# A 31-tap depthwise convolution moved from POOL to TensorE, and most of the weight splits moved from DVE to POOL

## The chip, the cores and the metric

One core of one Trainium2 chip runs the whole program. The metric is the device time of one execution in microseconds. The kernel before takes 1408.82 us (median of 3 runs, 1407.81 to 1412.9). DVE is VectorE, ACT is ScalarE, POOL is GpSimd, PE is TensorE, SP is the engine whose queue issues the transfers.

## What is computed

One transformer layer on 256 tokens of 1024 channels, all in float32: one input projection feeds three mixers (latent attention, a Mamba-2 scan, a convolution module), their outputs are gated, merged and projected, and then a mixture of 32 experts follows. The part that the change rewrites is the convolution module:

```python
CNV_CH, CNV_WIDTH, SEQ = 512, 31, 256

def _conformer_conv(a, gt, dw_w, dw_b, ln_g, ln_b):
    u = a * jax.nn.sigmoid(gt)
    u = _dwconv(u, dw_w, dw_b)          # each channel by its own 31 taps, centred
    return jax.nn.silu(_layernorm(u, ln_g, ln_b))
```

Every channel is filtered alone: out[c, t] = b[c] + sum over j of w[j, c] * u[c, t + j - 15].

## The kernel before

**The weights.** All matrices ahead of the experts are cut on the host into 696 blocks of 128x128, and eight blocks make a unit (`unit(u)`, 512 KB, 87 units). A unit is loaded into a `raw` buffer (three of them), copied by ACT into a rounded float32r half `wh` (L242), and the rest `wl` = raw - wh is taken by a subtraction of 128x1024 (L243), called a split below. L243 runs on DVE, or on POOL where the unit's number stands in `LOW_POOL` (17 units, the first is 47). `wh` and `wl` have three buffers each. PE then does three matmuls per block (L286 to L288: wh by the high half of the input, wh by its low half, wl by the high half).

**The order.** PE's order is written out by hand in `SEQ`: each word is one step, and a step that is named again goes on to its next phase. The other engines' instructions are ordered by a scheduler. Every engine runs its own list in order. The first part of SEQ holds the projections for the convolution (cnv), attention (cq, cqn, qk, att), the Mamba inputs (x), then the scan (ssd), the norms, the gates (g), the convolution's layer norm (conf) and the merged outputs (br). The order of the blocks follows SEQ, so the units do too.

**The convolution.** `do_cnv(c)` treats 128 channels (c from 0 to 3). Its first phase projects a, its second projects the gate and writes u into `ups` with 15 zeros on either side (L382, DVE). Then POOL does all 31 taps: one multiplication with bias (L384), and 30 times a product (L387) and a sum (L388), 128x256 each. The result, `cacc`, is first read by `do_conf` (`fold`, L356, on DVE).

**The experts.** While the mixers run, the first experts' weights are loaded into a ring of tiles (`do_pre`, sent between units). From about 420 us on, the 32 experts follow, with a megabyte per tile and 12 tiles per expert.

Of the kernel before, what the change touches and what calls it, by code (L numbers as in the profile page):

```python
# [18 lines left out]
P = 128  # L19
# [19 lines left out]
NR = (11, 12, 14, 18, 19)  # L39
SLOTS = (9, 10, *range(9), *range(11, NR[4]))  # L40
XK = 2
LOW_POOL = (47, 49, 50, 51, 52, 54, 55, 56, 58, 61, 64, 65, 70, 73, 74, 75, 80)
MANUAL = {mybir.EngineType.PE}

OFF = dict(cq=0, ckv=384, kr=640, z=672, xbc=1696, dt=3232, a=3264, g=3776,
# [5 lines left out]


SEQ = """
cnv0 cnv0 cq1 cq2 cnv1 cq4 cq0 cq3 cnv1 kr0 cqn0 cnv2 dt0 cqn0 cnv3 kr0 cqn0 cnv3 x1 qk2 qk0 x9
att0 x10 qk1 cnv2 v0 x0 att0 x5 qk3 dt0 x2 att1 att0 dt0 x11 att2 att1 x8 pre0 att1 x6 att3 att2
x4 x3 pre1 att2 att3 x7 mid0 att3 pre2 pre3 ssd0 z2 ssd0 ssd0 z1 z4 ssd0 ssd1 ssd1 z0 ssd1 g1 z5
z3 ssd1 nrm0 ssd2 nrm1 nrm0 ssd2 pre4 g1 g0 ssd2 g1 g0 nrm0 nrm1 z6 ssd2 ssd3 z7 g4 g3 nrm2 ssd3
nrm2 conf0 g4 pre5 pre6 conf0 nrm1 conf0 g2 g3 g0 conf0 ssd3 g2 conf0 g3 g5 ssd3 conf0 nrm3 g4
# [7 lines left out]
def _plan():  # L66
# [7 lines left out]

    for kind, i in ORDER + [("out", 0)]:
        ph = phase[kind, i] = phase.get((kind, i), -1) + 1
        if kind == "cnv":
            proj(OFF["ag"[ph]] + i * P)
        elif kind == "g":
# [46 lines left out]
def _vec_plan():  # L126
    n = 0
    for name, w in (("b_g", 4), ("b_z", 8), ("b_gc", 8), ("b_ga", 8), ("b_gs", 8), ("cw5", 60), ("cb5", 12),
                    ("cw31", 124), ("clg", 4), ("clb", 4),
                    ("b_a", 4), ("b_xbc", 12), ("b_cq", 3), ("b_ckv", 2), ("b_kr", 1), ("cb31", 4),  # L130
                    ("qn", 3), ("kvn", 2), ("sn", 8), ("sd", 8), ("bbc", 8), ("lng", 8), ("lnb", 8)):
        VEC[name] = (n, w)
        n += w
    return n
# [43 lines left out]
def tile_trunk(ctx, tc, xT_d, xn_d, wf_d, vec_d, row_d, rw_d, cst_d, cst2_d, rope_d, ln1_d, ln2_d,  # L178
# [137 lines left out]
    def tmp(name, shape=None, tag="t1", bufs=4, dt=F32, pool=None):  # L316
        return (pool or m1).tile(shape or [P, S], dt, tag=tag, name=name, bufs=bufs)

    ups, cpr = slot(5, "ups", [P, 4 * (S + 30) + 2 * S]), None
    ups, cpr = ups[:, 0:4 * (S + 30)].rearrange("p (c n) -> p c n", c=4), ups[:, 4 * (S + 30):]  # L320
    PO.memset(ups[:, :, 0:15], 0.0)
    PO.memset(ups[:, :, S + 15:S + 30], 0.0)
    cbc = slot(6, "cbc", [P, 8, S])
    cacc, bmat, cmat = cbc[:, 0:4], cbc[:, 4:6], cbc[:, 6:8]
    xps = [m0.tile([P, S + 4], F32, name=f"xp{c}") for c in range(3)]
# [1 line left out]
        PO.memset(u_[:, 0:2], 0.0)  # L327
        PO.memset(u_[:, S + 2:S + 4], 0.0)
    xs = slot(7, "xs", [P, 8, S])
    sz = slot(8, "sz", [P, 8, S])  # L330
    vkt = slot(4, "vkt", [P, 6 * S])
    vt = vkt[:, 0:4 * S].rearrange("p (c n) -> p c n", c=2)
    krr, tab = vkt[:, 4 * S:5 * S], vkt[:, 5 * S:6 * S]
# [39 lines left out]
    def do_cnv(c):  # L373
# [6 lines left out]
        A.activation(th, pg, AF.Tanh, bias=W("b_g", c), scale=0.5)  # L380
        up = ups[:, c]
        V.scalar_tensor_tensor(up[:, 15:S + 15], th, 1.0, at, op0=ALU.add, op1=ALU.mult)  # L382
        acc = cacc[:, c]
        PO.tensor_scalar(acc, up[:, 0:S], W("cw31", c * 31), W("cb31", c), op0=ALU.mult, op1=ALU.add)  # L384
        for j in range(1, 31):
            pr = cpr[:, j % 2 * S:(j % 2 + 1) * S]
            PO.tensor_tensor(pr, up[:, j:j + S], W("cw31", c * 31 + j).to_broadcast([P, S]), op=ALU.mult)  # L387
            PO.tensor_add(acc, acc, pr)  # L388

    def do_x(t):  # L390
        px = proj(f"px{t}")
# [91 lines left out]

    def do_z(t):
        pz = proj(f"pz{t}")
        th = tmp(f"zth{t}")
        A.activation(th, pz, AF.Tanh, bias=W("b_z", t), scale=0.5)
        zv = tmp(f"zv{t}")
        A.activation(zv, pz, AF.Identity, bias=W("b_z", t), scale=0.5)
        V.scalar_tensor_tensor(sz[:, t], th, 1.0, zv, op0=ALU.add, op1=ALU.mult)  # L490
# [137 lines left out]

    def do_norm(g):
        y = ys[g]  # L630
        V.tensor_mul(y, y, sz[:, 2 * g:2 * g + 2])
        sq = tmp(f"ysq{g}", [P, 2, S], tag="ysq", bufs=1, pool=m2s[0])
        A.activation(sq, y, AF.Square)
        V.tensor_add(sq[:, 0], sq[:, 0], sq[:, 1])
# [95 lines left out]
            eng.dma_start(t, wdn_v[e, (u - 8) // 2, u % 2])  # L730
        return t

    nx, m2s, ys, dts, gths, att, mx, late = [0], [], [], [], {}, {}, [], {}
    steps = dict(cnv=do_cnv, x=do_x, dt=do_dt, cq=do_cq, kr=do_kr, cqn=do_cqn, z=do_z, v=do_v, qk=do_qk,
                 att=do_att, mid=do_mid, ssd=do_ssd, nrm=do_norm, conf=do_conf, g=do_g, pre=do_pre, br=do_br)
    live = {}
# [752 lines left out]
def pack(inputs):  # L1489
# [22 lines left out]
    put("b_kr", np.concatenate([kr, _swap(kr), np.tile(b[OFF["dt"]:OFF["dt"] + NE], 2)])[:, None])  # L1512
    put("cw5", f["ssm_conv_w"][0].reshape(5, 12, P).transpose(2, 1, 0).reshape(P, 60))
    put("cb5", cols(f["ssm_conv_b"][0]))
    put("cw31", f["cnv_dw_w"][0].reshape(31, 4, P).transpose(2, 1, 0).reshape(P, 124))
    put("cb31", cols(f["cnv_dw_b"][0]))
    put("clg", cols(f["cnv_ln_g"][0]))
    put("clb", cols(f["cnv_ln_b"][0]))
# [40 lines left out]
```

## Time and profile before

| | |
|---|---|
| median of 3 runs | 1408.82 us |
| the profiled execution's own time | 1414.25 us |
| its span, first to last instruction | 1412.4 us |
| mean granted TensorE clock | 0.902 of full speed |
| busy: PE, DVE, ACT, POOL | 1169.7, 614.1, 328.1, 293.4 us |
| POOL's products and sums of the convolution (L387, L388) | 100.6 and 124.4 us |
| splits on DVE (72) and on POOL (17) | 98.9 and 41.6 us |
| moved by DMA | 456.39 MB, 323 GB/s over the span |

The span has two halves with different limits. Up to about 390 us the mixers run, with little DMA in the first 250 us. From about 420 us to the end the experts run, with the DMA engines busy 99% of the time at 414 to 416 GB/s. The averages above mix the two, so the views below are taken by stretches of the first half. An engine's busy time holds the time in which one of its instructions had started and was held up.

### The profile page before, as it was taken

What the parts mean: (1) busy time and instruction counts of PE and PEld (TensorE: products, weight loads), DVE (VectorE), ACT (ScalarE), POOL (GpSimd) and SP (SyncE); (2) the same over time, 40 slices, a digit from 0 to 9 for tenths busy, and PEclk for the clock granted to TensorE, in tenths of its full rate; (3) what the DMA queues carried; (4) which work ended last, traced back from release to release, by engine and by line L of the source; (5) the groups of instructions that cost most, each with busy time, mean ns of one, the idle gap of its engine ahead of it and who ended that gap; (6) DMA issues with size and microseconds to landing.
All of it is one profiled execution on the core that took longest, in us unless ns stands there. A gap on an engine that the chain in (4) does not pass through costs nothing. (4 is left out here: it accounts for less than half of the span.)

```text
span 1412.4 us, 20889 instructions
## 1 busy us (share of the span) xinstructions
PE 1169.7 (83%) x7635; PEld 620.8 (44%) x7635; DVE 614.1 (43%) x1245; ACT 328.1 (23%) x668; POOL 293.4 (21%) x293
## 2 busy tenths in 40 slices
PE   7797797899957987887888879898888888877875
PEld 7786687799822433233232324242322323212222
DVE  5999996877653233223323221323233322222213
ACT  5565563545421011101110010111001011000001
POOL 5999999543030000000000000000000000000000
PEclk9898888899968899999998998999989999987897
DMA  7342333467949878999999999997999999999991
GB/s 249 106 149 100 109 135 135 149 211 268 328 170 416 328 308 349 414 416 415 417 414 415 415 414 418 416 416 281 384 416 414 414 416 416 416 416 415 414 396 45
DMA packets 89496, 456.39 MB, mean 323 GB/s; under 512 B 8304, under 2 KB 8704, under 8 KB 58496
## 3 DMA queue, kind: packets, MB, share of 16 engines
q1 hardware_dynamic: 89344, 454.33, 81.3%
q8 instruction: 99, 1.62, 0.5%
q14 instruction: 53, 0.43, 0.1%
HBM read 453.25 MB, written 1.05 MB: 322 GB/s over the span
## 5 line engine op out<-in xcount | busy, mean ns | idle before, releaser
L1225 PE MATMUL pGS<-ew,xsm 128*32 128x512 f32 x1408 | 194.8, 694 | 23.8 <-DMA ew<-in_wgu_dram 12.1
L1448 POOL TENSOR_TENSOR xn<-xn,lb 128x256 f32<-128x256 f32 x4 | 2.8, 723 | 993.3 <-DVE xn L1436 993.3
L1215 PE MATMUL pGL<-ew,xg 128*64 128x512 f32 x832 | 203.3, 642 | 2.8 <-DMA ew<-in_wgu_dram 2.8
L1154 DVE TENSOR_TENSOR xn<-xn,pos 128x512 f32<-128x512 f32 x124 | 79.9, 684 | 221.2 <-PE pos L1150 218.8
L1143 DVE SCALAR_TENSOR_TENSOR yl<-pY,gsl,yh 128x512 fp32r<-128x512 f32 x35 | 26.3, 751 | 236.0 <-ACTq L1202 93.0
L1087 ACT ACTIVATE sg<-gv 128x256 f32<-128x256 f32 x48 | 20.0, 417 | 459.1 <-DVE gv L1086 458.3
L388 POOL TENSOR_TENSOR cbc<-cbc,ups 128x256 f32<-128x256 f32 x120 | 124.4, 1036 | 4.6
L1215 PEld LDWEIGHTS pGL<-ew,xg 128*64 128x64 f32 x832 | 66.2, 147 | 123.5 <-issue 112.1
L1225 PEld LDWEIGHTS pGS<-ew,xsm 128*32 128x32 f32 x1408 | 55.2, 123 | 141.9 <-issue 110.6
L243 DVE TENSOR_TENSOR wl<-raw,wh 128x1024 fp32r<-128x1024 f32 (+1 forms) x72 | 98.9, 1382 | 38.4 <-ACT wh L242 38.0
L1296 PE MATMUL pY<-ew,hT 128*32 128x512 f32 x704 | 91.3, 664 | 23.2 <-ACT hT L1282 21.9
L242 ACT CAST wh<-raw 128x1024 fp32r<-128x1024 f32 (+1 forms) x89 | 90.9, 1030 | 61.5 <-DMA raw<-in_wf_dram 20.5
L1265 PE MATMUL pY<-ew,hT 128*64 128x512 f32 x416 | 101.2, 643 | 0.0
L387 POOL TENSOR_TENSOR ups<-ups,vec 128x256 f32<-128x256 f32 x120 | 100.6, 857 | 0.0
L1150 PE MATMUL pos<-yh,sc 64*128 64x512 f32 x124 | 47.7, 513 | 31.9 <-DVE xn L1154 24.1
L1142 ACT ACTIVATE yh<-pY,gsl 128x512 fp32r<-128x512 f32 x35 | 24.1, 687 | 191.9 <-PE pY L1265 87.5
L1265 PEld LDWEIGHTS pY<-ew,hT 128*64 128x64 f32 x416 | 30.9, 147 | 61.5 <-issue 60.0
L1296 PEld LDWEIGHTS pY<-ew,hT 128*32 128x32 f32 x704 | 22.2, 120 | 77.7 <-issue 44.2
L1150 PEld LDWEIGHTS pos<-yh,sc 64*128 64x128 f32 x124 | 18.0, 189 | 83.5 <-DVE xn L1154 50.7
L1086 DVE TENSOR_SCALAR gv<-pGS 128x256 f32<-128x256 f32 x22 | 9.3, 425 | 103.7 <-PE pGS L1225 103.7
L1221 PE MATMUL pGS<-bgu_t,bl 128*32 128x512 f32 x176 | 24.3, 622 | 35.5 <-DVEq L1202 13.5
L243 POOL TENSOR_TENSOR wl<-raw,wh 128x1024 fp32r<-128x1024 f32 x17 | 41.6, 2451 | 52.6 <-ACT wh L242 52.6
(446 smaller groups left out, 2182.7 us busy)
## 6 DMA issues: line engine op xcount, KB each, us to landing
ew<-in_wgu_dram SPq DMA_DIRECT2D x241, 1024.0 KB, 19.9
ew<-in_wdn_dram SPq DMA_DIRECT2D x124, 1024.0 KB, 20.0
raw<-in_wf_dram SPq DMA_DIRECT2D x87, 512.0 KB, 3.9
ew<-in_wgu_dram SPq DMA_DIRECT2D x30, 512.0 KB, 7.0
ew<-in_wdn_dram SPq DMA_DIRECT2D x8, 512.0 KB, 5.2
xraw<-in_xT_dram SPq DMA_DIRECT2D x4, 256.0 KB, 5.4
xn<-in_xn_dram SPq DMA_DIRECT2D x2, 512.0 KB, 6.5
lnt<-in_ln_dram SPq DMA_DIRECT2D x2, 512.0 KB, 10.1
```

Source lines behind the costliest of these rows:

```text
L242: A.copy(h[:, b], raw[:, b])
L243: (PO if u in LOW_POOL else V).tensor_sub(l[:, b], raw[:, b], h[:, b].bitcast(F32))
L387: PO.tensor_tensor(pr, up[:, j:j + S], W("cw31", c * 31 + j).to_broadcast([P, S]), op=ALU.mult)
L388: PO.tensor_add(acc, acc, pr)
L1143: V.scalar_tensor_tensor(yl, pY, gsl, yh.bitcast(F32), op0=ALU.mult, op1=ALU.subtract)
L1150: T.matmul(pos[n], sc[r, c * P:(c + 1) * P], y[r], start=(start and i == 0), stop=(i == 1))
L1154: V.tensor_add(dst, dst, po)
L1215: T.matmul(pL[q][h * 64:(h + 1) * 64].rearrange("p (g n) -> p g n", g=2), xg[:, k, s_], quarter(wt[k], h, q), start=False, stop=(k == KT - 1))
L1221: T.matmul(grp(pS, g), bl[:, g * TINY:(g + 1) * TINY].bitcast(F32), bgu_t[:, q * 512:(q + 1) * 512].bitcast(F32), start=True, stop=False)
L1225: T.matmul(grp(pS, g).rearrange("p (g n) -> p g n", g=2), xs_[:, k], quarter(wt[k], h, q), start=False, stop=(k == KT - 1))
L1265: T.matmul(pY[0][n * 64:(n + 1) * 64], hT[b][:, j, h * CAP:(h + 1) * CAP], wt[KT + 2 * b + h][:, j, n * 512:(n + 1) * 512], start=False, s ...
L1296: T.matmul(grp(pY, 2 * n + j), hT[:, j, g * TINY:(g + 1) * TINY], w[:, j, n * 512:(n + 1) * 512], start=(j == 1 and (b, h) == (0, 0)), sto ...
```

## The change

The taps of the convolution go to PE, and the number of units that POOL splits goes from 17 to 56 of 87.

For each group of 128 channels: POOL forms `wdg`, 32 diagonal blocks of 32x32, as one product of 128x1024 (a constant pattern `rep` by the taps). In a third phase PE copies each 32 channels onto all four groups of 32 partitions, shifted by 0, 1, 2 and 3 samples (`cvr`, 16 matmuls of 284 columns with 32 output rows), and ACT copies these out of PSUM (`reps`, 4 copies of 128x284). In a fourth phase 32 matmuls (`cvy`, 256 columns, 32 output rows, the stationary operand a stack of four diagonals) add up all taps, and ACT writes `cacc` with the bias. SEQ names cnv four times per group in place of two. The tile `sz` is now allocated at the first z step, since its place in the ring holds `wdg` first.

```diff
-LOW_POOL = (47, 49, 50, 51, 52, 54, 55, 56, 58, 61, 64, 65, 70, 73, 74, 75, 80)
+LOW_POOL = tuple(u for u in range(3, 82) if u % 3 or u > 60 and u % 2)
-cnv0 cnv0 cq1 cq2 cnv1 cq4 cq0 cq3 cnv1 kr0 cqn0 cnv2 dt0 cqn0 cnv3 kr0 cqn0 cnv3 x1 qk2 qk0 x9
-att0 x10 qk1 cnv2 v0 x0 att0 x5 qk3 dt0 x2 att1 att0 dt0 x11 att2 att1 x8 pre0 att1 x6 att3 att2
+cnv0 cnv0 cq1 cq2 cnv0 cnv1 cnv0 cq4 cq0 cq3 cnv1 kr0 cqn0 cnv2 cnv1 dt0 cqn0 cnv1 cnv3 kr0 cqn0 cnv2
+x1 qk2 cnv2 qk0 cnv2 x9 att0 x10 qk1 cnv3 v0 x0 cnv3 att0 x5 cnv3 qk3 dt0 x2 att1 att0 dt0 x11 att2 att1 x8
+pre0 att1 x6 att3 att2
...
-        acc = cacc[:, c]
-        PO.tensor_scalar(acc, up[:, 0:S], W("cw31", c * 31), W("cb31", c), op0=ALU.mult, op1=ALU.add)
-        for j in range(1, 31):
-            pr = cpr[:, j % 2 * S:(j % 2 + 1) * S]
-            PO.tensor_tensor(pr, up[:, j:j + S], W("cw31", c * 31 + j).to_broadcast([P, S]), op=ALU.mult)
-            PO.tensor_add(acc, acc, pr)
+        PO.tensor_tensor(wdg, C("rep").unsqueeze(1).to_broadcast([P, 32, 32]),
+                         WR("cw31")[:, c * 32:(c + 1) * 32].unsqueeze(2).to_broadcast([P, 32, 32]), op=ALU.mult)
+        yield
+
+        for g in range(4):
+            pr = sm(f"cvr{c}{g}", [P, RW])
+            for s in range(4):
+                T.matmul(pr[s * 32:(s + 1) * 32], C("ident", g * 32, (g + 1) * 32), up[:, s:s + RW],
+                         start=True, stop=True)
+            A.copy(reps[g], pr)
+        yield
+
+        py = sm(f"cvy{c}", [P, S])
+        for m in range(8):
+            for g in range(4):
+                T.matmul(py[g * 32:(g + 1) * 32], wdg[:, g * 8 + m], reps[g][:, 4 * m:4 * m + S],
+                         start=(m == 0), stop=(m == 7))
+        A.activation(cacc[:, c], py, AF.Identity, bias=W("cb31", c), scale=1.0)
...
+        if not szs:
+            szs.append(slot(8, "sz", [P, 8, S]))
```

POOL's list at the start of the convolution, before (`ups` and `cbc` are u and the running sum):

```order
L384 TENSOR_SCALAR cbc_138<-ups_135,vec_80 128x256
L387 TENSOR_TENSOR ups_135<-ups_135,vec_80 128x256 x2
L388 TENSOR_TENSOR cbc_138<-cbc_138,ups_135 128x256 x2
L387 TENSOR_TENSOR ups_135<-ups_135,vec_80 128x256 x2
L388 TENSOR_TENSOR cbc_138<-cbc_138,ups_135 128x256 x2
```

and now (`cvs` holds the diagonals, `wl4` is the split of unit 4):

```order
L390 TENSOR_TENSOR cvs_136<-cst2_113,vec_80 128x1024
L247 TENSOR_TENSOR wl4_306<-raw4_303,wh4_305 128x1024
L247 TENSOR_TENSOR wl5_373<-raw5_370,wh5_372 128x1024
L247 TENSOR_TENSOR wl7_437<-raw7_434,wh7_436 128x1024
L390 TENSOR_TENSOR cvs_136<-cst2_113,vec_80 128x1024
L247 TENSOR_TENSOR wl8_469<-raw8_466,wh8_468 128x1024
```

The 244 instructions of 128x256 are gone, and instructions of four times the size, split after split, stand there.

PE's list at the norm of the attention's latents, before (`c0s` and `c3s` are column sums, `c0r` further down waits for what DVE makes of them, `pa3` is the projection of unit 11):

```order
L288 MATMUL pa2_602<-xh_82,wl10_606 128x256
L408 MATMUL pdt_635<-cst_61,kro_593 128x32 x2
L350 MATMUL c0s_666<-cst_61,c0f_598 128x1 x2
L350 MATMUL c3s_681<-cst_61,c3f_600 128x1 x2
L286 MATMUL pa3_696<-xh_82,wh11_699 128x256
```

and now:

```order
L292 MATMUL pa2_540<-xh_82,wl10_544 128x256
L397 MATMUL cvr10_573<-ups_135,cst_61 32x284 x4
L397 MATMUL cvr11_579<-ups_135,cst_61 32x284 x4
L397 MATMUL cvr12_585<-ups_135,cst_61 32x284 x4
L397 MATMUL cvr13_591<-ups_135,cst_61 32x284 x4
L427 MATMUL pdt_597<-cst_61,kro_531 128x32 x2
L357 MATMUL c0s_628<-cst_61,c0f_536 128x1 x2
L357 MATMUL c3s_643<-cst_61,c3f_538 128x1 x2
L405 MATMUL cvy1_658<-ups_135,cvs_136 32x256 x3
```

The copies of the second channel group stand ahead of the column sums and its taps behind them, with nothing but six small matmuls between the two.

## Rows read from the trace of the kernel before

**Rows 1.** Windows of core 0: stretch, its length, busy us of each engine, clock, DMA.

```profile
core 0: us, PE busy (x) PEld busy (x) DVE busy (x) ACT busy (x) POOL busy (x), PEclk, DMA share, GB/s
7.00:46.00 39.00, 38.74 (x300) 37.74 (x300) 26.41 (x35) 22.68 (x34) 29.12 (x29) 1.00 0.68 227
46.00:150.00 104.00, 84.66 (x561) 76.61 (x562) 103.28 (x161) 58.96 (x132) 102.04 (x109) 0.87 0.36 117
150.00:250.00 100.00, 78.80 (x558) 71.27 (x557) 84.77 (x150) 51.18 (x122) 97.88 (x111) 0.85 0.35 121
250.00:300.00 50.00, 44.15 (x348) 42.48 (x348) 42.85 (x79) 27.82 (x51) 24.81 (x13) 0.90 0.48 160
300.00:390.00 90.00, 87.06 (x639) 82.02 (x637) 62.05 (x123) 44.79 (x60) 24.62 (x14) 1.00 0.82 293
```

**Rows 2.** Waits from 15 to 250 us: who waited for whom, total, times, longest.

```profile
POOL cbc L384 <- DVE ups L382: 15.2, 1, 15.2
...
DVE cvf L356 <- POOL cbc L388: 7.3, 1, 7.3
```

**Rows 3.** PE's waits from 40 to 260 us, same columns.

```profile
PE ptx L577 <- DVE y L625: 9.9, 3, 6.6
PE pcs L595 <- ACT cb L572: 7.6, 1, 7.6
PE c0r L363 <- DVE c3w L294: 6.8, 1, 6.8
PE px L286 <- ACT pt L548: 4.8, 1, 4.8
PE psc L527 <- ACT pe L536: 3.6, 2, 2.7
PE cvmr L363 <- DVE cvm L649: 3.4, 1, 3.4
PE pm L350 <- DVE y2w L369: 3.2, 1, 3.2
```

**Rows 4.** DVE's groups by line, 15 to 246 us: busy us, mean ns, idle before.

```profile
L243 DVE TENSOR_TENSOR wl<-raw,wh 128x1024 fp32r<-128x1024 f32 x44 | 65.4, 1497 | 12.9 <-ACT wh L242 12.7
L398 DVE SCALAR_TENSOR_TENSOR xacc<-xp,vec,xacc 128x256 f32<-128x256 f32 x48 | 35.6, 746 | 0.5
```

**Rows 5.** Lines 243, 398, 690: shortest, median, longest ns, first and last start.

```profile
L243 DVE TENSOR_TENSOR wl<-raw,wh x72: 683/1226/2556, 4.9 to 375.6; 128x1024 fp32r<-128x1024 f32 x68, 128x512 fp32r<-128x512 f32 x4
...
L398 DVE SCALAR_TENSOR_TENSOR xacc<-xp,vec,xacc x48: 454/826/995, 66.6 to 158.6; 128x256 f32<-128x256 f32 x48
...
L690 DVE TENSOR_TENSOR th_gc<-th_gc,th_ga x8: 411/424/1716, 295.0 to 357.9; 128x256 f32<-128x256 f32 x8
```

**Rows 6.** POOL's groups by line, whole span.

```profile
L243 POOL TENSOR_TENSOR wl<-raw,wh 128x1024 fp32r<-128x1024 f32 x17 | 41.6, 2451 | 52.6 <-ACT wh L242 52.6
```

**Rows 7.** Timeline at 301 us: start, us, instruction.

```profile
301.18 2.63 POOL L243 TENSOR_TENSOR wl<-raw,wh 128x1024 fp32r<-128x1024 f32 x1
...
302.38 1.72 DVE L690 TENSOR_TENSOR th_gc<-th_gc,th_ga 128x256 f32<-128x256 f32 x1
```

**Rows 8.** DVE's groups by line, 246 to 400 us: two of ten that are stretched.

```profile
L666 DVE SCALAR_TENSOR_TENSOR uw<-uth,uw 128x256 f32<-128x256 f32 x4 | 3.7, 936 | 0.7 <-ACT uw L665 0.6
...
L291 DVE TENSOR_SCALAR y2w<-y2w 128x2 int32<-128x2 int32 x1 | 1.9, 1948 | 0.0
```

**Rows 9.** PE's timeline at 73 and at 662 us, equal matmuls merged.

```profile
73.03 1.91 PE L527 MATMUL psc<-kts,qts 128*128 128x256 f32 x8
...
662.40 1.50 PE L1225 MATMUL pGS<-ew,xsm 128*32 128x512 f32 x12
```

**Rows 10.** ACT's groups by line, 0 to 460 us: one PSUM copy.

```profile
L394 ACT ACTIVATE xp<-px,vec 128x256 f32<-128x256 f32 x12 | 5.6, 468 | 0.1
```

**Rows 11.** Waits from 0 to 460 us: PE for a split on POOL.

```profile
PE ybc L288 <- POOL wl L243: 1.1, 1, 1.1
```

**Rows 12.** Waits of the DMA queue, 0 to 470 us: expert loads (L727) for a tile.

```profile
SPq L727 <- PE pGS L1225: 30.4, 6, 25.5
```

More of the change, by code (lines that the diff above doesn't have):

```diff
@@ L76, in _plan @@
         ph = phase[kind, i] = phase.get((kind, i), -1) + 1
+        if kind == "cnv" and ph > 1:
+            continue
         if kind == "cnv":
@@ L128, in _vec_plan @@
     for name, w in (("b_g", 4), ("b_z", 8), ("b_gc", 8), ("b_ga", 8), ("b_gs", 8), ("cw5", 60), ("cb5", 12),
-                    ("cw31", 124), ("clg", 4), ("clb", 4),
+                    ("cw31", 128), ("clg", 4), ("clb", 4),
                     ("b_a", 4), ("b_xbc", 12), ("b_cq", 3), ("b_ckv", 2), ("b_kr", 1), ("cb31", 4),
@@ L158, in _consts @@
     add("slb", p[:, None] < p[None, :], 1)
+    add("rep", p[:, None] % 32 == np.arange(32)[None, :], 1)
     add("addm", (p[:, None] < 64) & (p[:, None] % 32 == p[None, :] % 32), 1)
@@ L317, in tmp @@
         return (pool or m1).tile(shape or [P, S], dt, tag=tag, name=name, bufs=bufs)
-    ups, cpr = slot(5, "ups", [P, 4 * (S + 30) + 2 * S]), None
-    ups, cpr = ups[:, 0:4 * (S + 30)].rearrange("p (c n) -> p c n", c=4), ups[:, 4 * (S + 30):]
+    UW, RW = S + 31, S + 28
+    upr = slot(5, "ups", [P, 4 * UW + 3 * RW])
+    cvs = slot(8, "cvs", [P, 1024 + RW])
+    ups = upr[:, 0:4 * UW].rearrange("p (c n) -> p c n", c=4)
+    reps = [upr[:, 4 * UW + i * RW:4 * UW + (i + 1) * RW] for i in range(3)] + [cvs[:, 1024:1024 + RW]]
+    wdg = cvs[:, 0:1024].rearrange("p (k c) -> p k c", c=32)
     PO.memset(ups[:, :, 0:15], 0.0)
-    PO.memset(ups[:, :, S + 15:S + 30], 0.0)
+    PO.memset(ups[:, :, S + 15:UW], 0.0)
     cbc = slot(6, "cbc", [P, 8, S])
@@ L329, in tile_trunk @@
     xs = slot(7, "xs", [P, 8, S])
-    sz = slot(8, "sz", [P, 8, S])
     vkt = slot(4, "vkt", [P, 6 * S])
@@ L485, in do_z @@
         pz = proj(f"pz{t}")
+        if not szs:
+            szs.append(slot(8, "sz", [P, 8, S]))
+        sz = szs[0]
         th = tmp(f"zth{t}")
@@ L630, in do_norm @@
         y = ys[g]
-        V.tensor_mul(y, y, sz[:, 2 * g:2 * g + 2])
+        V.tensor_mul(y, y, szs[0][:, 2 * g:2 * g + 2])
         sq = tmp(f"ysq{g}", [P, 2, S], tag="ysq", bufs=1, pool=m2s[0])
@@ L731, in load @@
         return t
-    nx, m2s, ys, dts, gths, att, mx, late = [0], [], [], [], {}, {}, [], {}
+    nx, m2s, ys, dts, gths, att, mx, late, szs = [0], [], [], [], {}, {}, [], {}, []
     steps = dict(cnv=do_cnv, x=do_x, dt=do_dt, cq=do_cq, kr=do_kr, cqn=do_cqn, z=do_z, v=do_v, qk=do_qk,
@@ L1514, in pack @@
     put("cb5", cols(f["ssm_conv_b"][0]))
-    put("cw31", f["cnv_dw_w"][0].reshape(31, 4, P).transpose(2, 1, 0).reshape(P, 124))
+    taps = np.concatenate([f["cnv_dw_w"][0], np.zeros((1, 512), np.float32)])
+    put("cw31", taps.reshape(8, 4, 4, 4, 32).transpose(1, 4, 2, 3, 0).reshape(P, 128))
     put("cb31", cols(f["cnv_dw_b"][0]))
```

## The prediction

> **What bounds the kernel now.** I read the page's slices first, to separate the mixers (to about 390 us) from the experts, then the windows of the mixers [rows 1]. The reader should see three regimes there. From 7 to 46 us PE is busy 38.7 of 39 us at full clock: PE is the limit. From 46 to 250 us PE works 80% of the time and its clock stands at 0.87 and 0.85, while DVE is busy 103.3 of 104 us in the first of the two stretches and POOL 97% and more in both. From 300 to 390 us PE is busy 97% again at clock 1.00, with DVE at 69%.
>
> So POOL's convolution is one continuous job from 15.2 us, when its first operand arrives, to shortly before 250 us, when the layer norm's first reduction on DVE has waited 7.3 us for it [rows 2]. It costs in two ways. It ends late, and it makes DVE slow: the same L398 takes 454 ns at its shortest and 746 ns on average in that stretch, and the split L243 1497 ns against a median of 1226 over the whole kernel [rows 4, 5]. The reason is visible at 301 us: DVE's L690, 0.42 us long by its median, takes 1.72 us and ends when POOL's split ends [rows 5, 7]. While POOL works on SBUF, a DVE instruction that works on SBUF alone stands still. PE in turn waits for DVE directly or through ACT: seven waits of 3.2 us and more add up to 39 us [rows 3].
>
> After the mixers the experts are limited by DMA, and their loads wait for ring tiles, up to 25.5 us, until the first expert's matmuls free one [rows 12]. What the mixers save therefore reaches the end in full: the expert half only moves.
>
> **The change part by part.** I take each stretch of rows 1 and ask how long it becomes.
>
> *The price of a chunk of convolution on PE.* Eight float32 matmuls of 256 columns, full width, take 1.91 us, the last one's drain included, so about 0.22 each; twelve with 32 output rows and 512 columns end within 1.50 us, three rounds of four, 0.43 a round and a drain [rows 9]. Four narrow matmuls thus run side by side for the price of one. A chunk has 4 rounds of 284 columns (0.24) and 8 of 256 (0.22): 2.7 us. If nothing ran side by side it would be 16 x 0.24 + 32 x 0.22 = 10.9 us. I take 3.0, near the row with the same 32 output rows, with a little for the changes of shape. ACT gets 5 PSUM reads per chunk of about 0.47 us [rows 10], 9 us in all; ACT is busy 58% or less of every stretch [rows 1], and where PE works on something else meanwhile they cost nothing.
>
> *The price of a split on POOL for DVE.* The split itself takes 2.45 us there [rows 6], against 1.2 on DVE. From 246 to 400 us, where POOL splits 17 units, ten groups of DVE instructions are stretched by 20 us in sum, from 0.94 us for one that is as large as L690 to 1.95 us for an operation on two elements [rows 8]. That is 1.2 us of DVE per POOL split. Bounds: 0, if DVE reads PSUM or waits anyway, and 2.45, if it always runs into the start of one. I take 1.2. A moved split then costs DVE what it saves; DVE's gain is the end of the convolution's interference, not the splits. POOL's four products of 128x1024 are priced as splits.
>
> *7 to 46 us.* Two chunks fall here, PE is full: +6 us (from +5 to +22).
>
> *46 to 150 us.* PE: 104, less its waits there (6.8 + 4.8 + 3.6 = 15 [rows 3]), less what the half clock costs. A mean of 0.87 means 27 us at the lower level, 1.2 in place of 2.4 GHz [rows 1]; some 7 of them are idle, half of the rest, 10 us, is lost. Plus two chunks, 6: 85 us. DVE: 103; of its 161 instructions about three quarters work on SBUF alone and lose 0.29 us each, as L398 does, 35 us; 12 of the splits go (-14), 14 POOL instructions of 1024 columns come (+17): 71 us. PE now limits. Since DVE still delays it at times I let PE be busy 92%, between the 88% of 250 to 300 us and the 97% after [rows 1]: 92 us, a gain of 12.
>
> *150 to 250 us.* PE: 100 less waits (9.9 + 7.6 + 3.2 = 21), less half clock (30 us at half speed, 8 of them idle, 11 lost): 68. DVE by the same reckoning: 85 - 33 - 13 + 13 = 52. Here the scan hands work from PE to ACT to DVE and back, so I let PE be busy 85%: 80 us, a gain of 20. The wait of 7.3 us at the end of the convolution is in it.
>
> *250 to 300 us.* The wait of 3.4 us for the layer norm's mean and the half clock that follows it (0.90) shrink, as that chain no longer starts late: a gain of 4, between 0 and 7.
>
> *300 to 390 us.* PE is full; no gain. But of units 47 to 81 POOL now splits 27 in place of 17, and PE has once waited 1.1 us for a split on POOL [rows 11]. Ten more: a loss between 0 and 11; I take 3, as sixteen of the seventeen did not make PE wait.
>
> Sum: -6 + 12 + 20 + 4 - 3 = 27 us off the profiled execution's own 1414.25 us (a span of 1412.4 and 1.9 around it), so 1387. The median of the runs is 5.4 us below that execution, and I take the same 27 off 1408.82: **1382 us**.
>
> **The skill against the row.** At 301 us DVE waits until POOL is through, and never once takes turns with it [rows 7]; the mean loss of 1.2 us per POOL split comes from DVE often being elsewhere. The Trainium skill, SBUF — State Buffer, section "SBUF: two separate sides", says more sharply that the pair of ports that POOL and DVE share is an exclusive lock: whoever starts first keeps it for a whole instruction and "the other fully blocks". By that rule a long POOL instruction is worse than many short ones, since a busy DVE runs into nearly every one and stands for most of it; that speaks against this change, and the second rival below is what it would give.
>
> **The rivals.**
>
> *Everything that DVE held up goes.* PE becomes the limit without gaps: 46 to 150 us becomes 85 (gain 19), 150 to 250 us 68 (gain 32), 250 to 300 us gains 7, no loss after, 6 paid before: 52 us, 1357. For it: PE does run at 97% where POOL is quiet for longer. Against: PE's waits in the scan go through ACT as well [rows 3], and POOL will be busy over a third of the time (14 x 2.45 of 92 us).
>
> *POOL's long splits hold DVE for their whole length.* At 2.45 per instruction DVE needs 88 us from 46 to 150 us, as much as PE's 85, and 66 beside PE's 68 after that. Both full: 96 and 85 us, gains of 8 and 15, then 2, and a loss of 8 in the last stretch, where 18 of 21 units in a row are POOL's: -6 + 8 + 15 + 2 - 8 = 11, so 1398. For it: rows 7. Against: the 1.2 of rows 8 is the measured mean, and DVE instructions that read PSUM go on meanwhile.
>
> *PE waits at each hand-off of the convolution, and it gets slower.* Eight times PE depends on a copy through ACT (u into the copies, the copies into the taps), and ACT works in order behind the weights' copies. One such wait now costs PE 4.8 us [rows 3]. Eight of those, 38 us, eat the 27 and leave +11: 1420. It decides from 27 / 8 = 3.4 us per hand-off. Against: SEQ puts 24 matmuls or more between most of them; only the second group's copies and taps stand six small matmuls apart, and there PE used to wait 6.8 us anyway.
>
> *The narrow matmuls don't run side by side.* Then a chunk costs 10.9, 32 us more in sum, on the stretches where PE is the limit: 1382 + 32 = 1414, within what can be told from no change. Against: rows 9.
>
> **How the numbers follow.** A difference under 0.5% (7 us) is about what a measurement of this kernel can't tell from none. Chances: my forecast (gains of 15 to 45 us) 0.66, all gaps gone 0.12, the full hold 0.13, hand-offs 0.05, narrow matmuls 0.04. The range leaves out the two last and a part of the first rival: 1356 to 1402. Faster by more than 0.5%: 0.66 + 0.12 + most of 0.13 = 0.88; the same 0.07; slower 0.05.
>
> **What would show each step.** In the profile of the changed kernel: PE still full up to about 52 us; L398's mean near 0.5 to 0.6 us, with a few instructions of over 2 us in place of many of 0.8; PE's waits between 50 and 250 us at half of 39 us or less, its clock above 0.9; the narrow matmuls starting in fours, a chunk in about 3 us; the first expert's matmuls some 27 us earlier, and the expert half as long as before. I am wrong if PE waits for ACT at the copies, if PE's waits for splits on POOL after 250 us add up to more than 10 us, or if DVE is still busy over 95% from 50 to 150 us.

## The result, and the profile after

The changed kernel takes 1392.22 us (median of 4 runs, 1388.9 to 1398.13), the kernel before beside it on the same chip 1410.17: a ratio of 0.9877, 95% interval 0.9837 to 0.9917. That is a gain of 17 to 18 us. It is faster, as forecast, and within the range given, but the forecast was a gain of 27. Each kernel has one profiled execution, so every figure read from a trace below is one sample; the medians stand beside it in the table.

The profiled execution has a span of 1391.6 us, 20.8 less than before. I measure the first half by the **start of the first expert**, the first matmul on the expert's biases. This view gives one line's shortest, median and longest duration and its first and last start:

```profile
L1243 PE MATMUL pGS<-bgu_t,bl x176: 589/593/1063, 391.1 to 1271.0; 128*32 128x512 f32 x176
```

and of the kernel before:

```profile
L1221 PE MATMUL pGS<-bgu_t,bl x176: 589/592/1061, 406.6 to 1291.8; 128*32 128x512 f32 x176
```

The kernel before starts its first expert at 406.6 us. So 15.5 us come from the mixers. The rest of the span, the experts, is 1000.5 us against 1005.8, but the runs below show 997 to 1009 us for that half with the same expert code, so these 5 us prove nothing.

The windows of the changed kernel, with the columns and stretches of [rows 1]:

```profile
core 0: us, PE busy (x) PEld busy (x) DVE busy (x) ACT busy (x) POOL busy (x), PEclk, DMA share, GB/s
7.00:46.00 39.00, 38.86 (x355) 35.57 (x356) 13.30 (x15) 21.64 (x34) 18.72 (x8) 1.00 0.62 205
46.00:150.00 104.00, 97.65 (x881) 83.26 (x879) 78.29 (x162) 64.51 (x148) 38.39 (x16) 0.98 0.39 129
150.00:250.00 100.00, 90.10 (x685) 81.15 (x686) 83.97 (x178) 62.75 (x147) 37.78 (x18) 0.95 0.46 158
250.00:300.00 50.00, 47.60 (x407) 46.31 (x406) 37.94 (x62) 25.41 (x42) 25.13 (x11) 1.00 0.56 191
300.00:390.00 90.00, 75.45 (x486) 68.24 (x485) 61.76 (x116) 40.91 (x56) 41.15 (x21) 0.90 0.70 254
```

PE now works 94% and 90% of the two stretches where it worked 81% and 79%, at 0.98 and 0.95 of full clock in place of 0.87 and 0.85. DVE, which had filled its first stretch (103.28 of 104 us), is at 78.29. POOL's load there falls from 102 to 38 us. The waits of PE in the seven lines of [rows 3], 39 us in sum, have become small. PE's waits from 40 to 260 us (who, for whom, total, times, longest):

```profile
PE ptx L599 <- DVE y L647: 2.6, 2, 1.5
PE py L641 <- DVE ef L628: 2.0, 1, 2.0
PE pcs L617 <- ACT cb L594: 2.0, 1, 2.0
PE po L576 <- ACT pt L570: 1.9, 1, 1.9
PE ptp L569 <- ACT xp L413: 1.9, 1, 1.9
PE px L292 <- DVE wl L247: 1.7, 1, 1.7
PE cvr L370 <- DVE cvw L299: 1.1, 1, 1.1
```

These seven sum to 13.2 us. (The `cvr` of L370 is the layer norm's, not a copy of the convolution.)

The same three lines as in [rows 5]: the split (L243, now L247), L398 (now L417) and L690 (now L712):

```profile
L247 POOL TENSOR_TENSOR wl<-raw,wh x56: 2362/2395/3014, 17.6 to 346.0; 128x1024 fp32r<-128x1024 f32 x56
L247 DVE TENSOR_TENSOR wl<-raw,wh x33: 683/1225/3402, 4.9 to 360.2; 128x1024 fp32r<-128x1024 f32 x29, 128x512 fp32r<-128x512 f32 x4
...
L417 DVE SCALAR_TENSOR_TENSOR xacc<-xp,vec,xacc x48: 466/485/2487, 67.2 to 156.6; 128x256 f32<-128x256 f32 x48
...
  ACT xth L419: 20.3, 8
...
L712 DVE TENSOR_TENSOR th_gc<-th_gc,th_ga x8: 408/616/2577, 272.3 to 343.9; 128x256 f32<-128x256 f32 x8
```

The pattern has turned over. Before, nearly every L398 was somewhat long (median 826 ns). Now the median is 485, and a few are held for up to 2487 ns. ACT, which waits for L417, has still spent 20.3 us on that (25.3 before).

What holds them is visible in the timeline, which gives start, duration, instruction. At 145 us, two L417 on DVE beside a split on POOL:

```profile
145.46 2.46 POOL L247 TENSOR_TENSOR wl<-raw,wh 128x1024 fp32r<-128x1024 f32 x1 [0.45 <-ACT wh L246]
...
145.21 3.00 DVE L417 SCALAR_TENSOR_TENSOR xacc<-xp,vec,xacc 128x256 f32<-128x256 f32 x2
```

The second of the two, which alone takes 0.48 us, ends at 148.21 us, 0.29 us behind the end of the split (147.92). The same at the end of the mixers:

```profile
339.52 2.39 POOL L247 TENSOR_TENSOR wl<-raw,wh 128x1024 fp32r<-128x1024 f32 x1 [2.56 <-ACT wh L246]
343.67 4.93 POOL L247 TENSOR_TENSOR wl<-raw,wh 128x1024 fp32r<-128x1024 f32 x2 [1.75 <-ACT wh L246]
...
339.99 2.21 DVE L712 TENSOR_TENSOR th_gc<-th_gc,th_gs 128x256 f32<-128x256 f32 x1
...
343.86 2.50 DVE L712 TENSOR_TENSOR th_gc<-th_gc,th_ga 128x256 f32<-128x256 f32 x1
346.27 0.41 DVE L711 SCALAR_TENSOR_TENSOR th_gs<-th_gs,yb_gs 128x256 f32<-128x256 f32 x1
346.72 2.17 DVE L712 TENSOR_TENSOR th_gc<-th_gc,th_gs 128x256 f32<-128x256 f32 x1
```

Each of these three L712, 0.41 us when nothing is in its way, begins inside a split on POOL and ends about 0.3 us behind the end of that split (at 341.9 us the first one, 342.2 the L712 in it). L711, which has one of its inputs in PSUM, needs 0.41 us beside a running split, and all sixteen of L711 take 402 to 422 ns. The Trainium skill, SBUF — State Buffer, section "Who interferes with whom", says as much: an instruction of DVE with two SBUF inputs contends with a POOL instruction that reads SBUF, one with at most one such input, outside DVE's two-port modes, does not. These rows agree.

The chunk of convolution on PE, in the timeline from 20.5 us (equal matmuls merged):

```profile
20.40 0.28 PE L291 MATMUL pc<-xl,wh 128*128 128x256 f32 x1
20.52 0.29 PE L292 MATMUL pc<-xh,wl 128*128 128x256 f32 x1
20.73 2.12 PE L397 MATMUL cvr<-ups,cst 128*32 128x284 f32 x32
22.79 0.39 PE L290 MATMUL pa<-xh,wh 128*128 128x256 f32 x1
...
25.83 0.42 PE L405 MATMUL cvy<-ups,cvs 128*32 128x256 f32 x3
25.85 0.40 PE L405 MATMUL cvy<-cvs 128*32 128x256 f32 x1
26.07 0.39 PE L405 MATMUL cvy<-ups,cvs 128*32 128x256 f32 x3
26.09 0.38 PE L405 MATMUL cvy<-cvs 128*32 128x256 f32 x1
```

The four narrow matmuls do start together (three and one in each round). But the 16 copies of a chunk stand as 32 records, and the 32 taps as 64 in 16 rounds 0.22 us apart: each float32 matmul leaves two records. Copies 1.95 us and taps 3.45: 5.4 us a chunk.

### The profile page after: what moved, and what is told of

It is laid out like the page before. It is cut to its first block, busy times and chain, and to the rows that moved or that the text cites. A ratio compares the mean times of both kernels' runs of the same rounds, so it can differ in the third digit from the quotient of the medians.

```text
span 1391.6 us, 21452 instructions
## 1 busy us (share of the span) xinstructions
PE 1176.0 (85%) x8019; PEld 618.2 (44%) x8019; DVE 560.1 (40%) x1206; ACT 332.4 (24%) x688; POOL 171.3 (12%) x92
## 3 DMA queue, kind: packets, MB, share of 16 engines
HBM read 453.27 MB, written 1.05 MB: 326 GB/s over the span
## 5 line engine op out<-in xcount | busy, mean ns | idle before, releaser
L1247 PE MATMUL pGS<-ew,xsm 128*32 128x512 f32 x1408 | 192.3, 684 | 23.1 <-DMA ew<-in_wgu_dram 11.4
L247 POOL TENSOR_TENSOR wl<-raw,wh 128x1024 fp32r<-128x1024 f32 x56 | 137.0, 2452 | 161.9 <-ACT wh L246 153.9
L246 ACT CAST wh<-raw 128x1024 fp32r<-128x1024 f32 (+1 forms) x89 | 91.1, 1028 | 57.1 <-DMA raw<-in_wf_dram 19.9
L1172 PE MATMUL pos<-yh,sc 64*128 64x512 f32 x124 | 47.9, 515 | 32.0 <-DVE xn L1176 23.9
L247 DVE TENSOR_TENSOR wl<-raw,wh 128x1024 fp32r<-128x1024 f32 (+1 forms) x33 | 43.7, 1328 | 44.5 <-ACT wh L246 44.4
L1210 ACT COPY xsm<-xg 128x256 f32<-128x256 f32 x32 | 12.9, 402 | 141.7 <-PE pGS L1247 131.4
L1108 DVE TENSOR_SCALAR gv<-pGL 128x256 f32<-128x256 f32 x26 | 11.0, 425 | 82.9 <-PE pGL L1237 81.8
```

What stands on the lines that cost most here:

```text
L246: A.copy(h[:, b], raw[:, b])
L247: (PO if u in LOW_POOL else V).tensor_sub(l[:, b], raw[:, b], h[:, b].bitcast(F32))
L1108: V.tensor_scalar_min(gv, ps[:, 0:256], LIMIT)
L1172: T.matmul(pos[n], sc[r, c * P:(c + 1) * P], y[r], start=(start and i == 0), stop=(i == 1))
L1247: T.matmul(grp(pS, g).rearrange("p (g n) -> p g n", g=2), xs_[:, k], quarter(wt[k], h, q), start=False, stop=(k == KT - 1))
```

## The experiments

All were run for what they tell of two questions. How much of the convolution's cost on PE is on the path? And what do POOL's splits cost, and by what? The column "first expert" is read as above. Each ratio is to the kernel before as it ran beside that kernel, on the same chip (medians of 1407 to 1412 us), so ratios, and not medians, compare two rows.

| kernel | convolution | splits on POOL | first expert, us | median, us | ratio to before, interval |
|---|---|---|---|---|---|
| before | POOL | 17 | 406.6 | 1408.82 | 1 |
| after | PE | 56 | 391.1 | 1392.22 | 0.9877 [0.9837, 0.9917] |
| e1 | PE | 17 | 364.2 | 1366.77 | 0.9708 [0.9653, 0.9764] |
| e2 | POOL | 56 | 495.8 | 1495.29 | 1.0601 [1.0541, 1.066] |
| e3 | PE, taps twice | 56 | 407.1 | 1410.57 | 0.9995 [0.9966, 1.0024] |
| e4 | PE | 56, in quarters | 381.9 | 1391.1 | 0.9875 [0.9821, 0.9928] |
| e5 | PE | 46 | 383.3 | 1387.91 | 0.9844 [0.978, 0.9907] |
| e6 | PE | none | 359.5 | 1364.68 | 0.9681 [0.9625, 0.9737] |
| e7 | POOL, 2 taps | 17 | 342.5 | 1728.59 (other routing) | 1.2263 [1.2192, 1.2334] |
| e8 | PE, copies by DMA | 17 | 392.6 | 1396.78 | 0.9918 [0.9886, 0.995] |
| e9 | PE | 17, and 29 idle | 404.7 | 1407.18 | 1.0006 [0.9974, 1.0038] |
| e10 | group 0 POOL, 1 to 3 PE | none | 363.9 | 1367.77 | 0.9708 [0.9654, 0.9763] |
| e11 | PE | 17, and 29 idle in quarters | 388.7 | 1394.05 | 0.9875 [0.9823, 0.9927] |

### The two halves of the change apart

**e1: the convolution on PE, the old list of splits.**

```diff
-LOW_POOL = tuple(u for u in range(3, 82) if u % 3 or u > 60 and u % 2)
+LOW_POOL = (47, 49, 50, 51, 52, 54, 55, 56, 58, 61, 64, 65, 70, 73, 74, 75, 80)
```

> The convolution on PE as in the changed kernel, the 17 units that POOL splits as in the kernel before. Theory (a split moved to POOL costs DVE about the 1.2 us that it saves it): within 4 us of the changed kernel, so ratio to before 0.985 to 0.991, and the loss of 5.5 us between the first ybc and the first pw gone, as POOL no longer splits nearly every unit there. Rival (the moved splits are what frees DVE): 8 us or more slower than the changed kernel, ratio 0.993 or above, with DVE over 90% busy from 50 to 150 us.

It is faster than either number: 1366.77 us, and the first expert starts 26.9 us ahead of the changed kernel's. The second half of the change costs what the forecast had hoped to gain in all. Its windows:

```profile
46.00:150.00 104.00, 101.82 (x936) 86.73 (x935) 82.75 (x198) 72.54 (x167) 3.84 (x2) 1.00 0.43 140
150.00:250.00 100.00, 94.82 (x785) 87.01 (x785) 86.22 (x185) 68.08 (x152) 24.83 (x13) 1.00 0.48 164
```

DVE is *busier* than in the changed kernel (82.75 and 86.22 against 78.29 and 83.97 us), and yet PE is fuller, 98% and 95%, at full clock. L417 tells why:

```profile
L417 DVE SCALAR_TENSOR_TENSOR xacc<-xp,vec,xacc x48: 466/480/490, 67.3 to 145.2; 128x256 f32<-128x256 f32 x48
...
  ACT xth L419: 3.8, 4
```

Its longest is 490 ns where the changed kernel has 2487, and ACT waits 3.8 us for it where it waits 20.3. So what the moved splits cost can't be read from DVE's busy time.

**e2: the new list of splits, the convolution on POOL.** The edit is the first line of the change's diff alone.

> The convolution stays on POOL as before, and POOL splits the 56 units of the changed kernel. POOL works on its list in order, so a split of an early unit stands behind or between up to 61 instructions of a convolution chunk, and PE waits for it. Theory: POOL needs its 230 us for the convolution and about 40 x 2.45 = 98 us more for the added splits in the first 250 us, and PE waits for both: slower than before by 40 to 100 us, ratio 1.03 to 1.07. Rival (the splits alone are a gain): ratio below 1.0.

6% slower. POOL works its list in order, and the splits stand behind taps. PE's longest waits from 15 to 340 us:

```profile
PE px L288 <- POOL wl L243: 35.5, 7, 13.6
PE pa L288 <- POOL wl L243: 14.5, 2, 7.9
PE pg L288 <- POOL wl L243: 14.1, 2, 11.1
```

Without the first half of the change the second costs 89.2 us at the first expert (495.8 less 406.6), and after it 26.9 (the changed kernel against e1). It is a gain in neither case.

### What the convolution costs on PE

**e3: the taps twice** (a loop of two around the 32 matmuls; the second pass starts its sums from zero, so the output is the same).

> The changed kernel with the 32 tap matmuls of each chunk done twice, the second time from zero, so the sums are the same. Theory (PE is the limit where the chunks stand, and a float32 matmul is two passes of 0.216 us for each four that run side by side): 16 rounds x 0.216 = 3.45 us per chunk, 13.8 us in all, of which 10 to 14 arrive at the first expert: ratio to the changed kernel 1.007 to 1.010. Rival (PE has slack there, what is late is late for DVE): under 4 us.

The first expert starts 16.0 us later than the changed kernel's. The added 64 records per chunk are 13.8 us by the price of 3.45 us read above, 4 chunks; the other 2.2 us are not explained. So the taps are on the path with their whole price. One record for each matmul would have added only 6.9 us (four times 8 rounds of 0.22).

**e7: no convolution to speak of.** The kernel before with 2 of 31 taps; the routing of the tokens differs with it, and so the expert half (1384 us from the first expert to the end), so only the first half is read.

```diff
-        for j in range(1, 31):
+        for j in range(1, 2):
```

> The kernel before with only 2 of the 31 taps: 29 products and 29 sums of each channel group on POOL are left out, nothing is put on PE. It measures what POOL's convolution costs the other engines in all. Theory (in the variant with the convolution on PE and the old list PE is the bound, and the four chunks of 5.4 us stand on the path): first expert at 364 - 22 = 342 us, 64 us ahead of the kernel before, ratio 0.954. Rival (hand-offs between engines set the pace and the chunks only fill PE's gaps): first expert at 358 us or later, ratio 0.966 or above.

342.5 us, as the theory has it: 21.7 us ahead of e1, and four chunks are 4 x 5.4 = 21.6. That fits a kernel in which PE is the bound and nothing of the convolution is hidden, as PE's 98% and 95% in e1 also say. The 29 taps left out cost the kernel before 406.6 - 342.5 = 64 us at the first expert.

**e8: the shifted copies by DMA, in place of matmuls and ACT's copies**, 16 transfers per chunk from ACT's queue, with the old list of splits.

```diff
-                T.matmul(pr[s * 32:(s + 1) * 32], C("ident", g * 32, (g + 1) * 32), up[:, s:s + RW],
-                         start=True, stop=True)
-            A.copy(reps[g], pr)
+                A.dma_start(reps[g][s * 32:(s + 1) * 32], up[g * 32:(g + 1) * 32, s:s + RW])
```

> Convolution on PE, the old list of POOL splits, and the shifted copies made by 16 transfers of 32x284 per channel group from ACT's queue, in place of 16 matmuls of PE and 4 copies of ACT. Theory (PE is the bound there): 1.95 us less PE work per channel group, 7.8 us in all, so the first expert at 356 to 359 us in place of 364 and a ratio of 0.965 to 0.967. Rival (issuing 64 transfers holds ACT, and the taps wait for their landing): first expert at 364 us or later, ratio 0.971 or above, and PE waits at the taps for a transfer.

The rival is right, and by more than it said: 28 us later than e1, 27 of them by the end of the last chunk's taps (131 us against 104). PE's waits from 7 to 80 us, and ACT's from 10 to 100:

```profile
PE pa L290 <- ACT wh L246: 7.6, 1, 7.6
...
PE cvy L402 <- DMA ups<-ups: 3.4, 3, 1.6
PE cvy L402 <- DMA cvs<-ups: 1.5, 1, 1.5
```

```profile
ACT ee L429 <- DMA cvs<-ups: 6.0, 1, 6.0
ACT qts L529 <- DMA cvs<-ups: 5.3, 1, 5.3
...
ACT wh L246 <- DMA cvs<-ups: 5.1, 1, 5.1
```

The transfers sit in ACT's list ahead of the rounding of weights (L246), which PE needs next and once waits 7.6 us for. The taps themselves wait 12.8 us for transfers in the whole of the convolution (to 200 us). Saving 7.8 us of PE was not worth the two. Copies from another queue, or asked for earlier, were not tried.

### What a split on POOL costs

**e5: only the late units back on DVE** (POOL keeps the change's list below unit 60 and the old list from 60 on).

> The changed kernel, but from unit 60 on POOL splits only the 8 units that it split before; below 60 the change's list stands. Theory (every split moved to POOL costs about the same, 27 us for 39 moved ones): the ten taken back are worth 7 us, so the first expert starts at about 384 us in place of 391 and the time is about 1385, ratio to the kernel before 0.982. Rival (in the last stretch PE is full and DVE has room, a POOL split there costs nothing): first expert at 390 to 392 us and a ratio of 0.987 as for the change.

The theory's figure (384) is met with 383.3 in the trace; by the medians (0.9844 and 0.9877, intervals that overlap) the two kernels can't be told apart. Up to the first of the conv branch's output matmuls (261 us) the two kernels keep step; from there to the end of the merged outputs it takes 76.2 us in place of 82.4. The waits `PE yb_gs <- POOL wl` of 2.9 us and `PE pg_gc <- POOL wl` of 1.4, which the changed kernel has after 250 us, are gone, with 1.2 us of waits for DVE's splits in their place. So ten splits in the last stretch cost 7.8 us, and the other 29 (net) the remaining 19.1 to e1.

**e6: no split on POOL.**

```diff
-LOW_POOL = tuple(u for u in range(3, 82) if u % 3 or u > 60 and u % 2)
+LOW_POOL = ()
```

> The changed kernel with no split on POOL at all; POOL is left with four products for the diagonals and small work. Theory (a POOL split costs the chain of mixers 0.7 us, 27 / 39): the 17 that the kernel before had on POOL are worth about 12 us, the first expert starts at about 352 us where the variant with the old list has 364, ratio 0.962. Rival (from unit 47 on DVE is the tighter engine, and 17 splits of 1.2 us more make it the bound): first expert at 364 us or later, ratio 0.971 or above.

4.7 us ahead of e1, between the two. By the medians (0.9681 and 0.9708, intervals that overlap) the two can't be told apart. By the traces the old 17 cost 0.3 us each, the 39 added by the change 0.7. That e6 needs no POOL for splits shows that DVE had room for all 89: it was never the 98.9 us of splits that had made DVE late, but the convolution beside them. With 1364.68 us, e6 has the lowest time of all.

**e4: each split on POOL as four of 128x256.**

> The changed kernel with each split on POOL made as four instructions of 128x256 in place of one of 128x1024. Theory (a DVE instruction waits only for the POOL instruction that is running, and PE is the limit anyway): DVE's longest waits fall from 2.5 to about 0.8 us, POOL's splits grow from 2.45 to about 2.9 us each, and the time moves by less than 4 us either way. Rival (the length of the hold is what DVE and so PE pay for): 6 to 15 us faster than the changed kernel, by the gaps that PE still has from 50 to 235 us, 15 us.

The first expert starts 9.2 us earlier, although the quarters keep POOL busy longer (50 in place of 38 us in each of the two middle stretches). The rival's range holds the trace. But that execution, at 1380.72 us, is the fastest of its five by 10 us, and the medians, 1391.1 against 1392.22, show no gain. So this run leaves open what quarters are worth; e11 below answers it.

**e9: idle splits.** Every split that e1 has on DVE stays there; POOL computes 29 of them a second time, into a tile that nobody reads.

```diff
+                if u in IDLE_POOL:
+                    PO.tensor_sub(idle[0], raw, h.bitcast(F32))
```

> Convolution on PE, the old list of POOL splits, so every split stands where it stood in the variant with a first expert at 364.2 us; on top POOL computes 29 splits (units 4 to 46, two of three) a second time into a tile that nobody reads before it is overwritten. Nobody waits for POOL's result; POOL's access to SBUF is the only thing added, apart from raw and wh buffers that stay taken until POOL has read them. The list that stops at unit 60 has the first expert at 383.3 us, 19 us later. Theory (POOL's splits hold up DVE, whoever needs their result): first expert at 378 to 386 us, L417 with a longest of 2.4 us, ratio to the kernel before 0.980 to 0.986. Rival (the 19 us come from the splits being delivered later, since POOL takes twice as long and keeps its list's order): first expert at 364 to 368 us, ratio 0.971 to 0.974.

404.7 us: work that nobody waits for costs 40.5 us at the first expert, 1.4 for each idle split, and the whole gain over the kernel before is gone. The late delivery of the rival can't be it: of PE's waits from 40 to 260 us the longest name the scan's chains through ACT and DVE, and only 1.6 us in all are for a `wl`:

```profile
PE ptx L604 <- DVE y L652: 9.4, 3, 4.5
PE pcs L622 <- ACT cb L599: 5.2, 2, 5.0
PE ptp L574 <- DVE pe L566: 2.2, 1, 2.2
```

and L422, which is the changed kernel's L417, is held as it is there, for up to 2617 ns, while POOL's own splits are stretched too, 2348 ns at the shortest and 4355 at the longest:

```profile
L251 POOL TENSOR_TENSOR cvh<-raw,wh x29: 2348/3052/4355, 18.5 to 243.0; 128x1024 fp32r<-128x1024 f32 x29
```

The theory's number, 378 to 386, was too low because DVE still does the splits here. The buffers that the idle splits hold don't explain it either. The loads into `raw` do wait for them, 31.1 us in 14 waits of at most 2.2, but ACT, which needs these loads, waits only 0.4 us for one between 15 and 260 us, and 1.6 us for an idle split. What grows is DVE's work on SBUF alone:

```profile
L566 DVE TENSOR_TENSOR pe<-pe,sums 128x512 f32<-128x512 f32 x8 | 9.2, 1170 | 0.1
...
L607 DVE TENSOR_TENSOR xd<-ptx,dtv 128x256 f32<-128x256 f32 x16 | 5.6, 408 | 0.0
```

In e1 the first of these takes 687 ns on average (L561 there) and the second, which has an input in PSUM, 415 (L602). ACT's rounding keeps its 1.05 us in both.

That gives the balance which the prediction had guessed: 29 splits on POOL cost some 40 us, and taking the same 29 off DVE gives back some 21 (40.5 less the 19.1 of e5, which moves them).

**e11: the idle splits in quarters.**

> The same 29 idle splits on POOL, each as four instructions of 128x256. Theory (it is the length for which POOL keeps DVE out at a time that hurts, since it lands on chains from PE over ACT and DVE back to PE): about two thirds of what the whole ones cost, as quartering took 9 of 27 us off the change; L417 with a longest near 1.1 us; first expert 5 us or more ahead of the whole idle splits. Rival (the amount of POOL work counts, not the length of one piece): first expert within 2 us of the whole idle splits, or later, since four quarters keep POOL busy a third longer.

388.7 us: 24.5 us over e1 where whole ones cost 40.5, though POOL is busy for 121.7 us with them in place of 85.7. L417 is at most 960 ns long there (2617 with whole ones). The medians agree (1394.05 against 1407.18, intervals of the ratios apart). The length of the single hold hurts more than the amount of work. Whether all of the 24.5 us are holds is not shown: ACT waits 9.2 us for loads into `raw` in e11 (0.4 in e9), and the loads wait for POOL's quarters too, 69.9 us in 25 waits.

**e10: the first channel group on POOL, where DVE has slack.** Groups 1 to 3 as in the change, all splits on DVE; group 0 as in the kernel before, the diagonals of group 2 formed by DVE.

```diff
+        if c == 0:
+            diag(PO, 1)
+            acc = cacc[:, 0]
+            PO.tensor_scalar(acc, up[:, 0:S], W("cw31f", 0), W("cb31", 0), op0=ALU.mult, op1=ALU.add)
+            for j in range(1, 31):
+                pr = cacc[:, 2 + j % 2]
+                PO.tensor_tensor(pr, up[:, j:j + S], W("cw31f", j).to_broadcast([P, S]), op=ALU.mult)
+                PO.tensor_add(acc, acc, pr)
```

> Splits all on DVE, channel groups 1 to 3 on PE as in the change, group 0 on POOL as before (61 instructions of 128x256 from about 15 to 71 us), the diagonals of group 2 formed by DVE. Theory (POOL's work costs little where DVE has slack; from 7 to 46 us DVE is busy half the time and PE is full): PE is spared 5.4 us, DVE loses some of it after 46 us: first expert at 355 to 359 us in place of 359.5, ratio 0.963 to 0.968. Rival (a piece of POOL work delays the chains wherever it runs): first expert at 365 us or later, ratio 0.972 or above.

Neither: 363.9, between the theory's 359 and the rival's 365. The first 46 us are indeed shorter by the chunk (PE's first matmul into `pkk`, the mark that ends the first stretch below, starts at 50.6 us in place of 56.2). From 46 to 80 us it is lost again (e10, then e6):

```profile
46.00:80.00 34.00, 29.37 (x276) 24.66 (x269) 31.12 (x57) 17.14 (x38) 28.54 (x35) 0.90 0.23 72
...
46.00:80.00 34.00, 34.00 (x370) 27.40 (x370) 23.39 (x69) 22.10 (x49) 3.84 (x2) 1.00 0.37 111
```

DVE is busy 31.12 of 34 us there (23.39 in e6), PE 29.37 (34.00 in e6), and PE's clock stands at 0.90. So POOL's work cost nothing from 7 to 46 us, where DVE was busy 25.12 of 39 us, and it cost the chunk's gain and 4.4 us more behind that.

## Why the prediction was right, and which terms were off

**The forecast's sum, step by step.** The lengths run between marks in PE's work near the ends of the stretches of [rows 1]: the first matmuls into `pkk` (45.2 us before, 56.6 after), `pcb` (149.3, 152.2), `pm` (249.7, 233.4), `ybc` (283.3, 261.4) and the first expert (406.6, 391.1).

| stretch | forecast | measured |
|---|---|---|
| 7 to 46 us, two chunks | +6 | +11.4 |
| 46 to 150 us | -12 | -8.5 |
| 150 to 250 us | -20 | -19.2 |
| 250 to 300 us | -4 | -5.6 |
| 300 to 390 us and up to the first expert | +3 | +6.4 |
| sum | -27 | -15.5 |

**The price of a chunk was mis-sized.** I took 3.0 us, and it is 5.4: 9.6 us in four chunks, where the sum missed 11.5 in all. The error lies in how [rows 9] were read. The row `psc x8` was taken for eight matmuls in 1.91 us, 0.22 each. But the program has four there (two loops of two around L527): a float32 matmul stands in the trace as two records. The second row was misread in the same way, its twelve records being six matmuls. My bounds of 2.7 to 10.9 held the price, though the upper one was halved by the same slip, and the corrected price follows from the same row: 12 rounds at two records of 0.22 to 0.24. The Trainium skill, FP8 and Floating Point Precision, section "TensorE Precision Notes", states that true FP32 takes four passes through the array; the float32r matmuls of 256 columns above start 0.12 us apart (20.40 and 20.52 us), a float32 one takes 2 x 0.22, so the trace agrees with a factor near four.

With 5.4 in place of 3.0 the forecast would have been 27 - 9.6 = 17.4 us at the first expert. The trace shows 15.5, the medians some 18.

**By parts of the change three terms were off, and that they nearly cancel is luck.** The forecast's terms add up to 42 us for what POOL's convolution had held up (the gains of 12, 20 and 4, and the 6 that two chunks take from the first of them), -12 for four chunks on PE, and -3 for the moved splits. The runs show 64.1 (e7), -21.7 (e1 against e7) and -26.9 (the changed kernel against e1). So the first was 22.1 us too low, the second 9.7 and the third 23.9 too mild, and 22.1 - 9.7 - 23.9 is the -11.5 of the sum. The moved splits, which the prediction held to be neutral for DVE and PE but for 3 us, took back most of what the convolution's move gave.

**The stretches came out, their reasons only in part.** PE still limits from 7 to 46 us and its first stretch grows by two chunks (11.4 and 2 x 5.4). I had let PE be busy 92% and 85% in the two middle stretches; between the marks it was 92% (88.1 of 95.6 us) and 91% (74.1 of 81.2). In the second, PE's own work was put at 68 us and is 74, which the better filling made up. DVE's busy time came out for the first (71.7 us, 71 forecast) and not for the second (66.9, 52 forecast). I had put PE's gaps in the second down to the scan's hand-offs. But e1, with the same hand-offs, is at 99% and 96% between its marks: more than half of the gaps came with the moved splits. Of the signs that the prediction named, the few L417 of over 2 us, the waits at a third of 39 us and the clock above 0.9 came; L417's mean of 629 ns is a little above the 0.5 to 0.6 us named, and a chunk takes 5.4 us, not about 3. One row was misread without effect: the 15.2 us of [rows 2] is the length of POOL's wait; its first L384 starts at 16.3 us.

**300 to 390 us.** The mechanism was right, the size half of what it is: ten more splits on POOL cost 7.8 us by e5, taken at 3. My argument, that sixteen of seventeen had not made PE wait, looked only at waits for the splits themselves, and the cost can come also by way of L712, which holds up what PE multiplies next.

**The price of a split for DVE** was right as busy time and wrong as a price. I wrote that a moved split costs DVE what it saves, 1.2 us either way. On the path it costs 1.4 us (e9) and gives back about 0.7 (21 us for 29). The likely reason is that DVE is not full from 46 us on (78 of 104 us), so 1.2 us off its load is worth less than that, while a hold of 2.4 us can fall on a chain PE, ACT, DVE, PE. Part of this loss stood, unnoticed, in the allowances of 92% and 85%.

**The rivals.** *Everything that DVE held up goes* is not what the change does, but it is e1: 52 us of gain forecast for it, less the 9.6 of the chunks, is 42.4, and e1's first expert starts 406.6 - 364.2 = 42.4 us earlier. By stretches the two differ by up to 5 us either way, so that the sums agree to the tenth is chance. What stands between the change and that rival is the second half of the change. *The full hold* was right about the single hold (2.2 to 2.5 us in the rows above) and about the last stretch, where it named a loss of 8 and e5 shows 7.8. Its sum (11 us, less 9.6) did not come: DVE at 78 of 104 us is not full. *Hand-offs*: PE's only wait at the copies or taps is one of 0.7 us. *Narrow matmuls one after another*: they start together.

The Trainium skill, Perfetto Trace Analysis, section "Optimizing Scalar/DVE Operations", warns that moving work between POOL and DVE might not help, since they share a port. Here the move of 39 splits cost 27 us (e1 against the changed kernel); the warning was the thing to weigh for that half of the change by itself.

**What stays open.** Why the old 17 late splits cost 0.3 us each and ten more there 0.8 isn't settled, and both figures are differences of single traces: the later ones could fall more often on L712, but that was not tried by itself. And in e9 PE's waits from 40 to 260 us sum to 30.5 us against 7.3 in e1, which is 23 of the 40.5 us; the lower clock (0.88 from 150 to 250 us, 1.00 in e1) is part of the rest, and how the rest divides is not shown.

## What to carry to other kernels

A change in two halves wants a price for each half by itself: here one was worth 42 us and the other cost 27. Before a matmul is priced from a row, count the program's matmuls behind its records; a float32 one left two here. And work on POOL is priced by the time for which it can hold a DVE instruction that stands in a chain, not only by the busy time that it adds; where it must be there, short pieces cost less than long ones (e11 against e9).

## What the runs showed of the hardware

- A float32 matmul of 256 columns is two records of 0.22 us (psc, cvy), whether 128 or 32 output rows wide; four of 32 rows on different groups start within 0.02 us of each other.
- POOL work that nobody needs can cost as much as a whole optimization: 29 splits, 85.7 us of POOL's time, made the first expert 40.5 us later. DVE's L417 grew from at most 490 ns (e1) to 2617 (e9), and POOL's split from 2.39 us by the median (the changed kernel) to 3.05 (e9), which fits that the two hold each other up.
- The same work in quarters costs 24.5 us, with L417 at no more than 0.96 us, while POOL is busy 42% longer.
- DVE instructions with an input in PSUM took no longer beside POOL's splits: L711 402 to 422 ns in the changed kernel, L602 415 ns on average in e1 and 408 in e9.
